# The low halves of the S5 layer's weights by an accumulating DMA instead of a VectorE subtraction

## The chip, the cores and the metric

The kernel runs on one core of one Trainium2 chip. The metric is the device time of one execution in microseconds. The kernel before takes 1155.73 us (median of 3 runs, 1154.44 to 1156.47).

## The reference

A trunk of four layers on 256 tokens of width 1024, all in float32. Each layer is a token mixer and then a SwiGLU feed-forward block, both behind an RMS norm and with a residual add. The mixers are forgetting attention (layer 0), a diagonal state-space layer called S5 (layer 1), multi-scale pooling (layer 2), and forgetting attention again (layer 3). Only layer 1 is touched here:

```python
def s5_layer(h, w_in, ..., w_glu):
    u = (h @ w_in).astype(F32)                      # 1024 x 1024
    bu = jnp.einsum('gpc,bsgc->bsgp', b_bar, u_g)   # 64 groups of 16 channels, 64 states each
    _, states = lax.associative_scan(combine, (lam_seq, bu), axis=1)
    y = jnp.einsum('gcp,bsgp->bsgc', c_mat, states).real.reshape(B, S, D_MODEL)
    g = jax.nn.gelu(y + d * u)
    val, gate = jnp.split(g @ w_glu, 2, axis=-1)    # 1024 x 2048
    return val * jax.nn.sigmoid(gate)
```

## The kernel before, in words

Activations lie with channels on the 128 partitions and the 256 tokens in the free dimension. TensorE multiplies in a fast float32 format (fp32r) that keeps fewer bits, so each operand is split into a rounded high half and a low half that holds the rest; a product is three matmuls: high by high, low by high, high by low (`term`).

All large weights stream through SBUF in **units** of 128 x 1024 float32 (512 KB), in one list over the whole program (`unit_list`). Each unit goes through three steps:

- `fetch` starts a DMA from SP's queue into one of 4 `raw` buffers;
- `split_unit` rounds `raw` on ScalarE into the first half of one of 5 `hl` buffers (the high half), and VectorE subtracts that half from `raw` into the second half (the low half);
- the matmuls on TensorE read `hl`.

`unit` is called when the code comes to the matmuls of a unit. It records the fetches up to 3 units ahead (`DMA_AHEAD`) and the splits up to 2 units ahead (`CAST_AHEAD`). A step can run only when its buffer is free: a `raw` buffer when the last reader of its former unit is done, an `hl` buffer when TensorE is done with the unit five places before.

The order of instructions on each engine is fixed when the program is built, by the language's scheduler, which may place an instruction ahead of others recorded before it; each engine then runs its list in order. Work between the matmuls (norms, the state-space steps) is put off by `at` and brought in by `tick`, which the matmul loops call.

The S5 layer has 24 units: 8 for `w_in` (`w_s5`), 4 for the first quarter of the GLU matrix (`w_glu0`, consumed while the state-space cores finish) and 12 for the rest of it (`w_glu1`). Units 0 and 1 are multiplied together, alternating over the 8 pieces of the inner dimension. While units 2 to 7 and the first GLU units are multiplied, eight state-space **cores** (`core`, `emit`) run between them: each needs three tables that an earlier preparation wrote to HBM (`E` 512 KB, `tab` 384 KB, `par` 768 KB, loaded by SP in `tables`), matmuls on TensorE (`e`, then `tp`) and eleven VectorE instructions on 256 to 512 elements. The last 12 units alternate value and gate: after each pair ScalarE takes the sigmoid of the gate, VectorE multiplies and adds to the residual, and `settled` makes the piece `X` and the squares `s` for the next norm.

Before the layer, the preparation of the tables ends in the feed-forward block of layer 0; its last pieces (`pe`, `pk`) leave through GpSimd's DMA queue. GpSimd also raises the norms' sums to the power -1/2 (L243) and loads the pooling layer's band matrix.

Of the kernel before, what the change touches and what calls it, by code (L numbers as in the profile page):

```python
# [9 lines left out]
F32 = mybir.dt.float32  # L10
F32R = mybir.dt.float32r
AF = mybir.ActivationFunctionType
ALU = mybir.AluOpType
# [13 lines left out]
CAST_AHEAD = 2  # L27
# [6 lines left out]
class Trunk:  # L34
# [21 lines left out]
    def units(self):  # L56
        a, u = self.a, []

        def ffn(l):
            for i in range(NCH):  # L60
                u.extend((a["w_gu"][l, i, 0], a["w_gu"][l, i, 1]))
            for d in range(8):
                u.extend(a["w_dn"][l, d][:, s] for s in (slice(0, 1024), slice(1024, 2048), slice(2048, 2816)))

        for l in range(self.layers):
            kind, j = l % 3, l // 3
            if kind == 0:
                u.extend(a["w_vf"][j, k] for k in range(8))
                for hp in range(8):
                    u.extend((a["w_qk"][j, hp, 0], a["w_qk"][j, hp, 1]))  # L70
                u.extend(a["w_fo"][j, k] for k in range(8))
            elif kind == 1:
                u.extend(a["w_s5"][m] for m in range(8))
                u.extend(a["w_glu0"][k] for k in range(4))
                u.extend(a["w_glu1"][d] for d in range(12))
            else:
                u.extend((a["w_pool"][:, 0:1024], a["w_pool"][:, 1024:2048]))
            ffn(l)
        self.unit_list = u
# [12 lines left out]
    def split_unit(self, h):  # L92
        nc = self.nc
        raw, cuts = self.raw.pop(h)
        hl = self.wp.tile([128, 2, 1040], F32R, tag="hl", name="hl", bufs=HL_BUFS)
        for p in range(len(cuts) - 1):
            s = slice(cuts[p], cuts[p + 1])
            nc.scalar.copy(hl[:, 0, s], raw[:, s])  # L98
            nc.vector.tensor_tensor(out=hl[:, 1, s], in0=raw[:, s], in1=hl[:, 0, s].bitcast(F32), op=ALU.subtract)  # L99
        self.hl[h] = hl  # L100

    def unit(self):
        h = self.used
        self.used += 1
        last = len(self.unit_list) - 1
        while self.fetched <= min(h + DMA_AHEAD - 1, last):
            self.fetch(self.fetched)
            self.fetched += 1
        while self.cast <= min(h + (CAST_AHEAD if h else 0), last):
            self.split_unit(self.cast)  # L110
            self.cast += 1
        return self.hl.pop(h)
# [905 lines left out]
```

## Time and profile before

| | |
|---|---|
| median of the runs | 1155.73 us |
| the profiled execution | 1157.62 us |
| its span, first to last instruction | 1155.8 us |
| TensorE, VectorE, ScalarE, GpSimd busy | 97%, 75%, 59%, 11% of the span |
| loads from SP's queue (hardware) | 200.86 MB, 54.3% of the 16 DMA engines |
| transfers from GpSimd's queue (software) | 22.00 MB, 5.8% |
| granted TensorE clock | 0.99 |

The S5 layer lies between about 341 and 450 us of the span. In the table of windows each engine has its busy time and, in brackets, its number of instructions; then come the granted clock, the mean busy share of the 16 DMA engines and what they moved in GB/s. In the rows of groups and of the timeline a line such as L99 is the line in the kernel's code; `hl<-raw,hl` names what is written and what is read; the last bracket tells how long the engine had been idle and what ended that. L156 is the helper through which all matmuls go.

### The profile page before, as it was taken

Reading aid. Unit: us, or ns where it says so; the run is one execution under the profiler, and the core shown is the slowest. Engines: PE = TensorE matmul, PEld = TensorE weight load, DVE = VectorE, ACT = ScalarE, POOL = GpSimd, SP = SyncE. Lnnn points to the kernel's source line nnn. Section 1 sums busy time; section 2 is a strip of 40 time slices with the busy share of each in tenths; the row PEclk is TensorE's granted clock in tenths of the full one; section 3 lists DMA queues with packets and bytes.
Section 4 is the critical chain, followed back from the end, with each engine's and each line's share of the span. In section 5 each row is a group of like instructions: output and inputs, shape, how many; then the busy total and the mean of one; then the engine's idle time right before and its main releaser. Section 6 shows DMA issues by size and latency. Waiting matters only on the chain. (4 is left out here: it accounts for less than half of the span.)

```text
span 1155.8 us, 22388 instructions
## 1 busy us (share of the span) xinstructions
PE 1119.3 (97%) x8706; PEld 1027.9 (89%) x8706; DVE 868.6 (75%) x1647; ACT 683.7 (59%) x1273; POOL 121.5 (11%) x167
## 2 busy tenths in 40 slices
PE   7979999999999999999999899999999999999997
PEld 6968999999999999888888888888898998888886
DVE  5979976798769975988756688876755667887763
ACT  5557755777753254766644676665545677666551
POOL 1176000111110000000000000000005720000000
PEclk9989999999999999999999999999999999999999
DMA  8654466788889744665566265556665544655661
GB/s 287 203 163 153 155 209 196 239 264 253 259 267 332 292 137 158 219 190 193 176 181 190 92 192 191 190 184 184 196 196 180 180 134 148 205 193 186 180 188 49
DMA packets 63210, 224.98 MB, mean 195 GB/s; under 512 B 7648, under 2 KB 7984, under 8 KB 62976
## 3 DMA queue, kind: packets, MB, share of 16 engines
q1 hardware_dynamic: 56368, 200.86, 54.3%
q0 software_dynamic: 6160, 22.00, 5.8%
q8 instruction: 68, 1.11, 0.4%
q10 hardware_dynamic: 576, 0.69, 0.2%
q14 instruction: 38, 0.31, 0.1%
HBM read 208.81 MB, written 14.71 MB: 193 GB/s over the span
## 5 line engine op out<-in xcount | busy, mean ns | idle before, releaser
L156 PE MATMUL P<-X,hl 128*128 128x256 f32 (+1 forms) x4560 | 678.1, 308 | 3.4 <-DVE t L183 2.0
L156 PEld LDWEIGHTS P<-X,hl 128*128 128x128 f32 x4560 | 618.2, 190 | 52.7 <-issue 6.9
L99 DVE TENSOR_TENSOR hl<-raw,hl 128x1024 fp32r<-128x1024 f32 (+3 forms) x363 | 434.7, 1199 | 143.0 <-ACT hl L98 134.9
L98 ACT CAST hl<-raw 128x1024 fp32r<-128x1024 f32 (+3 forms) x363 | 372.3, 1028 | 162.3 <-PE acc L156 75.5
L156 PE MATMUL acc<-H,hl 128*128 128x512 f32 (+1 forms) x1628 | 251.1, 315 | 0.0
L156 PEld LDWEIGHTS acc<-H,hl 128*128 128x128 f32 x1628 | 226.6, 188 | 21.1 <-issue 0.6
L182 ACT COPY lo<-P 128x256 f32<-128x256 f32 x126 | 46.8, 372 | 107.8 <-PE P L156 107.8
L183 DVE TENSOR_TENSOR t<-P,lo 128x256 f32<-128x256 f32 x126 | 53.2, 424 | 44.4 <-ACT lo L182 44.3
L156 PE MATMUL acc<-X,hl 128*128 128x256 f32 (+1 forms) x384 | 61.3, 300 | 0.1
L409 POOL TENSOR_SCALAR nb<-nb,c 128x128 f32<-128x128 f32 (+1 forms) x64 | 59.6, 945 | 1.1
L243 POOL TENSOR_TENSOR rs<-rs,mhalf 128x2 f32<-128x2 f32 x9 | 6.6, 735 | 469.5 <-DVE rs L242 469.5
L156 PEld LDWEIGHTS acc<-X,hl 128*128 128x128 f32 x384 | 50.5, 188 | 3.7 <-DVE X L194 0.3
L430 ACT ACTIVATE pt<-pt,st 128x128 f32<-128x128 f32 (+1 forms) x64 | 28.6, 448 | 24.5 <-DVE st L428 24.3
L278 ACT ACTIVATE t<-t 128x256 f32<-128x256 f32 x88 | 36.8, 419 | 8.1 <-DVE t L277 4.7
L156 PE MATMUL P<-hl,X 128*128 128x336 f32 (+1 forms) x192 | 40.4, 330 | 0.0
L208 ACT ACTIVATE X<-x,gains 128x256 fp32r<-128x256 f32 x55 | 27.7, 506 | 12.9 <-DVE x L263 12.3
L217 ACT ACTIVATE s<-x 128x256 f32<-128x256 f32 x63 | 25.6, 406 | 15.7 <-DVE x L263 13.1
L156 PEld LDWEIGHTS P<-hl,X 128*128 128x128 f32 x192 | 33.5, 197 | 0.0
L156 PE MATMUL acc<-hl,X 128*128 128x352 f32 x96 | 24.5, 338 | 8.6 <-DVE X L206 7.6
L209 DVE SCALAR_TENSOR_TENSOR X<-x,gains,X 128x256 fp32r<-128x256 f32 x56 | 26.8, 480 | 5.4 <-ACT X L208 5.3
L280 DVE TENSOR_TENSOR t<-t 128x256 f32<-128x256 f32 x66 | 28.0, 424 | 1.9
L277 DVE TENSOR_TENSOR t<-t,R 128x256 f32<-128x256 f32 x66 | 28.0, 424 | 1.7
(179 smaller groups left out, 852.9 us busy)
## 6 DMA issues: line engine op xcount, KB each, us to landing
raw<-in_w_gu SPq DMA_DIRECT2D x176, 512.0 KB, 3.7
raw<-in_w_dn SPq DMA_DIRECT2D x64, 512.0 KB, 3.7
raw<-in_w_qk SPq DMA_DIRECT2D x32, 512.0 KB, 3.6
raw<-in_w_dn SPq DMA_DIRECT2D x32, 384.0 KB, 3.2
raw<-in_w_fo SPq DMA_DIRECT2D x16, 512.0 KB, 4.3
raw<-in_w_glu SPq DMA_DIRECT2D x16, 512.0 KB, 5.5
raw<-in_w_vf SPq DMA_DIRECT2D x15, 520.0 KB, 4.3
nb<-nd POOLq DMA_DIRECT2D x24, 256.0 KB, 6.3
```

The source lines that it names most:

```text
L98: nc.scalar.copy(hl[:, 0, s], raw[:, s])
L99: nc.vector.tensor_tensor(out=hl[:, 1, s], in0=raw[:, s], in1=hl[:, 0, s].bitcast(F32), op=ALU.subtract)
L156: self.nc.tensor.matmul(out, lhsT=lhsT, rhs=rhs, start=start, stop=stop)
L182: nc.scalar.copy(lo, o[:, N:])
L183: nc.vector.tensor_tensor(out=t, in0=o[:, 0:N], in1=lo, op=ALU.add)
L208: nc.scalar.activation(self.X[:, d, 0], x, AF.Identity, scale=g)
L209: nc.vector.scalar_tensor_tensor(out=self.X[:, d, 1], in0=x, scalar=g, in1=self.X[:, d, 0].bitcast(F32), op0=ALU.mult, op1=ALU.subtract)
L277: nc.vector.tensor_tensor(out=t, in0=t if wide else G, in1=R, op=ALU.mult)
L278: nc.scalar.activation(t, t, AF.Silu)
L280: nc.vector.tensor_tensor(out=h, in0=h if wide else U, in1=t, op=ALU.mult)
L409: nc.gpsimd.tensor_scalar(out=nb[:, i], in0=nb[:, i], scalar1=self.c[t][:, 4 * n + i:4 * n + i + 1], scalar2=None, op0=ALU.add)
L430: nc.scalar.activation(pt, pt, AF.Exp, bias=st[:, 0:1], scale=-1.0, accum_out=st[:, 1:2])
```

## The change

For the 24 units of the S5 layer the low half is formed in another way. ScalarE rounds as before; then ScalarE writes the negated rounded half into the low half's place (an activation with scale -1); then GpSimd issues a DMA that adds the unit's raw weights, read once more from HBM, to what stands there. The subtraction on VectorE goes away for these units. Their splits are recorded 3 instead of 2 units ahead. For all other units nothing changes.

```diff
+        self.added = ()
         for l in range(self.layers):
...
                 u.extend(a["w_s5"][m] for m in range(8))
                 u.extend(a["w_glu0"][k] for k in range(4))
                 u.extend(a["w_glu1"][d] for d in range(12))
+                self.added = range(len(u) - 24, len(u))
...
             nc.scalar.copy(hl[:, 0, s], raw[:, s])
-            nc.vector.tensor_tensor(out=hl[:, 1, s], in0=raw[:, s], in1=hl[:, 0, s].bitcast(F32), op=ALU.subtract)
+            if h in self.added:
+                nc.scalar.activation(hl[:, 1, s], hl[:, 0, s].bitcast(F32), AF.Identity, scale=-1.0)
+                nc.gpsimd.dma_start(hl[:, 1, s], self.unit_list[h][:, s].bitcast(F32R), accum_op=ALU.add)
+            else:
+                nc.vector.tensor_tensor(out=hl[:, 1, s], in0=raw[:, s], in1=hl[:, 0, s].bitcast(F32),
+                                        op=ALU.subtract)
...
-        while self.cast <= min(h + (CAST_AHEAD if h else 0), last):
+        while self.cast <= min(h + (CAST_AHEAD + (self.cast in self.added) if h else 0), last):
```

The change also moves instructions. The code grows by seven lines, so L98 (rounding) becomes L100, L208 and L217 become L215 and L224, L243 becomes L250, L708 and L710 become L715 and L717, and L826 becomes L833; the negation is L102 and the accumulating DMA L103.

GpSimd at the layer's start, before. `pe` and `pk` are the last pieces of the tables, `sx` the cleared states, `rs` the norm's power, `band` the pooling matrix of the next layer.

```order
L718 DMA s5d7_88<-pe_4309 128x512
L710 DMA s5d7_88<-pk_2311 128x512
L782 MEMSET sx0_4509 128x8
L782 MEMSET sx1_4510 128x8
L243 TENSOR_TENSOR rs_4504<-rs_4504,mhalf_75 128x2
L470 DMA band_6096<-in_band 128x1088
```

And now; hl_4415, hl_4449, hl_4479, hl_4524 and hl_4530 are units 0 to 4.

```order
L725 DMA s5d7_88<-pe_4309 128x512
L103 DMA hl_4415<-in_w_s5 128x1024
L717 DMA s5d7_88<-pk_2311 128x512
L103 DMA hl_4449<-in_w_s5 128x1024
L103 DMA hl_4479<-in_w_s5 128x1024
L103 DMA hl_4524<-in_w_s5 128x1024
L789 MEMSET sx0_4515 128x8
L789 MEMSET sx1_4516 128x8
L250 TENSOR_TENSOR rs_4510<-rs_4510,mhalf_75 128x2
L103 DMA hl_4530<-in_w_s5 128x1024
```

The accumulations of units 0 to 3 now stand ahead of the norm's power, that of unit 1 behind the write of `pk`.

ScalarE at the same place, now (before, the rounding of unit 1 is followed by the same `pk` copies, `X` and `s`, and there are no negations):

```order
L100 CAST hl_4415<-raw_4410 128x1024
L102 ACTIVATE hl_4415<-hl_4415 128x1024
L100 CAST hl_4449<-raw_4447 128x1024
L715 COPY pk_2311<-tp_4386 32x4x32 x4
L215 ACTIVATE X_3700<-x_72,gains_74 128x256
L224 ACTIVATE s_4406<-x_72 128x256
L102 ACTIVATE hl_4449<-hl_4449 128x1024
L100 CAST hl_4479<-raw_4477 128x1024
L102 ACTIVATE hl_4479<-hl_4479 128x1024
```

The negation of unit 1 stands behind the copies of `pk` and the activations of the last pieces of the feed-forward block.

TensorE at the first pair of units, where `tp<-cst,sq` is the norm's sum and `tp<-cst,rs` spreads its result; before:

```order
L156 MATMUL P<-X,hl 128x256 x26
L156 MATMUL tp<-cst,sq 128x1 x2
L156 MATMUL P<-X,hl 128x256 x4
L249 MATMUL tp<-cst,rs 128x128 x2
L156 MATMUL P<-X,hl 128x256 x18
```

and now:

```order
L163 MATMUL P<-X,hl 128x256 x20
L163 MATMUL tp<-cst,sq 128x1 x2
L163 MATMUL P<-X,hl 128x256 x10
L256 MATMUL tp<-cst,rs 128x128 x2
L163 MATMUL P<-X,hl 128x256 x18
```

The norm's sum stands six matmuls earlier. Everywhere else the order of TensorE's instructions is the same as before.

## The prediction

> **What bounds the kernel now.** I read the stretch of the S5 layer first, in the view of busy time by windows, with cuts at the places where its work changes kind: the end of the feed-forward block before it, the first pair of weight units, two stretches with the state-space cores, the first GLU units, the last GLU units.
>
> ```profile
> core 0: us, PE busy (x) PEld busy (x) DVE busy (x) ACT busy (x) POOL busy (x), PEclk, DMA share, GB/s
> 320.00:341.00 21.00, 21.00 (x190) 20.67 (x189) 12.58 (x19) 11.60 (x18) 2.17 (x4) 1.00 0.82 250
> 341.00:352.00 11.00, 10.03 (x130) 9.38 (x129) 6.96 (x12) 4.20 (x6) 0.87 (x3) 1.00 0.96 363
> 352.00:372.00 20.00, 20.00 (x413) 18.93 (x411) 19.02 (x36) 6.43 (x8) 0.00 (x0) 1.00 0.88 304
> 372.00:395.00 23.00, 22.90 (x466) 21.47 (x468) 22.86 (x42) 7.10 (x10) 0.00 (x0) 1.00 0.96 357
> 395.00:415.00 20.00, 19.85 (x392) 18.49 (x389) 15.10 (x27) 6.46 (x10) 0.00 (x0) 1.00 0.39 130
> 415.00:450.00 35.00, 35.00 (x294) 34.82 (x294) 25.73 (x41) 21.39 (x36) 0.66 (x2) 1.00 0.55 170
> ```
>
> From 341 to 450, 109 us, TensorE is idle for 1.2 us in all. VectorE is nearly full from 352 to 395 (41.9 of 43 us), and so are the DMA engines from 341 to 395 (shares 0.96, 0.88, 0.96). ScalarE has room, GpSimd is idle. Which of the full ones sets the pace is told by what TensorE waits for, so I then read TensorE's waits from 325 to 455.
>
> ```profile
> PE tp L249 <- POOL rs L243: 0.9, 2, 0.5
> PE e L156 <- DVE u L789: 0.3, 1, 0.3
> PE tp L156 <- DVE sq L220: 0.2, 1, 0.2
> ```
>
> 1.4 us in all, at the norms' ends and once at the first core. TensorE does not wait for a subtraction (hl, L99) anywhere in the layer, though VectorE is full: VectorE keeps up. So there is almost nothing to win, and what matters is what the new form of the low half costs elsewhere.
>
> **The change part by part.**
>
> *Removed: 24 subtractions on VectorE.* The groups of 341 to 395 price one at 1.22 us, the ScalarE rounding beside it at 1.05 us.
>
> ```profile
> L99 DVE TENSOR_TENSOR hl<-raw,hl 128x1024 fp32r<-128x1024 f32 x10 | 12.1, 1221 | 2.5 <-ACT hl L98 2.4
> L98 ACT CAST hl<-raw 128x1024 fp32r<-128x1024 f32 x10 | 10.4, 1047 | 20.4 <-DMA raw<-in_w_s 7.5 <-PE acc L156 7.3 <-DMA raw<-in_w_glu 3.0
> ```
>
> 24 x 1.22 = 29 us leave VectorE, none of it on TensorE's path but one. At the first norm a subtraction stands ahead of the last X and sq.
>
> ```profile
> 342.36 1.23 DVE L99 TENSOR_TENSOR hl<-raw,hl 128x1024 fp32r<-128x1024 f32 x1
> 343.90 0.42 DVE L220 TENSOR_TENSOR sq<-sq,s 128x256 f32<-128x256 f32 x1
> 341.02 3.20 PE L156 MATMUL P<-X,hl 128*128 128x256 f32 x26
> 344.46 0.58 PE L156 MATMUL tp<-cst,sq 128*128 128x1 f32 x4 [0.23 <-DVE sq L220]
> 346.09 0.43 PE L249 MATMUL tp<-cst,rs 128*128 128x128 f32 x2 [0.47 <-POOL rs L243]
> ```
>
> Without it sq is ready up to 1.1 us sooner, and the new order puts the norm's sum after 20 matmuls instead of 26 and 10 behind it instead of 4, so the gaps of 0.23 and 0.47 can close: at best -0.7 us.
>
> *Added on ScalarE: 24 negations of 128x1024.* No such instruction is in the trace. These rows of the last GLU units bound it:
>
> ```profile
> 443.15 0.39 ACT L826 ACTIVATE s<-P 128x256 f32<-128x256 f32 x1 [1.75 <-PE P L156]
> 443.43 1.04 ACT L98 CAST hl<-raw 128x1024 fp32r<-128x1024 f32 x1
> 444.49 0.51 ACT L208 ACTIVATE X<-x,gains 128x256 fp32r<-128x256 f32 x1
> 444.90 0.40 ACT L217 ACTIVATE s<-x 128x256 f32<-128x256 f32 x1
> 446.02 1.05 ACT L98 CAST hl<-raw 128x1024 fp32r<-128x1024 f32 x1 [0.71 <-ACT s L217]
> 448.80 0.39 ACT L826 ACTIVATE s<-P 128x256 f32<-128x256 f32 x1 [1.74 <-PE P L156]
> ```
>
> An activation of 256 elements costs 0.40 or, with a vector as scale, 0.51; the rounding of 1024 costs 1.05. I take 1.05 (1.30 by the ratio 0.51 to 0.40). Over two GLU units (443.15 to 448.80, 5.65 us) ScalarE then holds 0.39 + 2 x 1.05 + 0.51 + 0.40 + 2 x 1.05 = 5.5 us: just enough, and 6.0 at the upper price, too much by 0.35 per pair.
>
> *Added on GpSimd and the DMA engines: 24 accumulating transfers.* Each reads the 512 KB of raw weights from HBM a second time, reads the 512 KB of the negated half, writes 512 KB. The trace has none, so I bound it by loads. Share and rate of a saturated stretch, 341 to 352:
>
> ```profile
> GB/s 432 343 75 0 223 60 119 149 179 402 410 372 439 391 413 436 480 380 402 402 462 402 402 417 402 432 454 365 391 425 451 413 369 458 458 425 358 425 492 402
> q1 hardware_dynamic: 990, 3.97, 95.0%
> ```
>
> The last 31 slices average 417 GB/s, so 0.524 MB take 1.26 us of all 16 engines; by busy share (95.0% of 11 us for 3.97 MB) 1.38 us. Lower bound for one accumulate: one such load. Upper: three, one for each stream. I take two, 2.5 to 2.8 us, since both operands must be read. The nearest rows for the time from issue to landing are GpSimd's own transfers:
>
> ```profile
> s5d<-cxv POOLq DMA_DIRECT2D x8, 512.0 KB, 4.5
> bc<-in_s_bc POOLq DMA_DIRECT2D x1, 1024.0 KB, 7.9
> ```
>
> 4.5 us is the lower end (same bytes written), 7.9 the one I take (the bytes read are the same).
>
> In the Trainium skill, Collectives: The Full Stack, section "The bandwidth ceiling: the fold count and why AG ≠ RS ≠ AR", a DMA that adds is said to run at half the rate of a copy, because it fetches two operands through the one read ring, the addition itself being free. No run shown so far tests it; it would give two loads per accumulate too, against one if only the bytes written counted.
>
> *The sum, first place: the S5 layer's start.* Units 0 and 1 feed one interleaved pair that starts at 341.02.
>
> ```profile
> 332.71 1.05 ACT L98 CAST hl<-raw 128x1024 fp32r<-128x1024 f32 x1 [1.07 <-PE acc L156]
> 335.17 0.40 ACT L217 ACTIVATE s<-x 128x256 f32<-128x256 f32 x1
> 335.58 0.54 POOL L710 DMA_DIRECT2D s5d<-pk  x1 [7.16 <-DVE pk L526]
> 345.32 0.72 POOL L243 TENSOR_TENSOR rs<-rs,mhalf 128x2 f32<-128x2 f32 x1 [3.91 <-DVE rs L242]
> ```
>
> Unit 1 is rounded at 332.71, but in the new order the four pk copies, X and s stand between its rounding and its negation: that runs 335.6 to 336.6, and GpSimd, in order, has pk's write (335.58) ahead of it. Issued at 336.6 it lands at 341.1 (4.5) or 344.5 (7.9); it is wanted at 341.4, three matmuls after 341.02. Late by 0 to 3.1 us, of which the 0.7 of gaps are taken back: -0.7 to +2.4, I take +2. The norm's power stays undisturbed: units 1 to 3 are issued ahead of it on GpSimd, the last at about 342, and it runs at 345.32.
>
> *Second place: DMA time from 341 to 450.* 21 accumulates fall here (24 less units 0 to 2). By bytes: 11 x 363 + 20 x 304 + 23 x 357 + 20 x 130 + 35 x 170 = 26.8 MB, 64.3 us at 417 GB/s; plus 42 x 1.26 = 52.9 makes 117.2 us of work in 109: 8 over. By busy share: 0.96 x 11 + 0.88 x 20 + 0.96 x 23 + 0.39 x 20 + 0.55 x 35 = 77.3, so 31.7 free against 42 x 1.38 = 58: 26 over. About 5 us can go past 450 (four raw buffers of 1.26). So +3 to +21. I take +7, nearer the low end, because the quoted slices swing between 358 and 492 GB/s under a full share: the share fills before the bytes do. It shows at two points. The tables' loads (E, tab, par) come late:
>
> ```profile
> 351.65 0.32 SPq L834 DMA_DIRECT2D E<-s5d  x1
> 361.18 2.01 PE L156 MATMUL e<-u,E 32*128 32x64 f32 x64
> E<-s5d SPq DMA_DIRECT2D x3, 512.0 KB, 6.3
> ```
>
> E is issued at 351.65 and wanted at 361.18, 9.5 us, against 6.3 to land (372 to 395): only 3 us spare. And the last GLU units: TensorE eats one in 2.85 us (below), the DMA engines need 1.26 + 2.5 = 3.8.
>
> ```profile
> 415.54 33.23 PE L156 MATMUL P<-X,hl 128*128 128x256 f32 x280
> 363.13 0.97 PE L156 MATMUL acc<-X,hl 128*128 128x256 f32 x6
> 366.21 3.10 PE L156 MATMUL acc<-X,hl 128*128 128x256 f32 x24
> 369.24 1.01 PE L156 MATMUL e<-u,E 32*128 32x64 f32 x28
> SPq L87 <- DVE hl L99: 62.0, 21, 7.0
> ```
>
> (33.23 / 280 x 24 = 2.85.) Casting one unit further ahead adds nothing here: five hl buffers hold the lead at four units either way. The last row is SP's wait for raw buffers; they now come free at the rounding, so raw loads start sooner, which costs nothing but meets the tables' loads.
>
> Sum: +2 + 7 = +9 us. The profiled execution took 1157.62 us (span 1155.8 and 1.8 around it) and would take 1166.6; it lies 1.9 above the median of the runs, 1155.73, so the forecast is 1164.7.
>
> **The rivals.**
>
> *Hidden, no change (0.27).* An accumulate costs the engines what a load costs: 21 x 1.38 = 29 of 31.7 us free, everything lands within its lead. For it: between two cores (361.18 to 369.24, 8.1 us) TensorE uses 6 + 24 = 30 matmuls of weights, 1.25 units, so a lead of four units is 26 us there. Against: shares of 0.96. Time: 1155.7 with -0.7 to +2 at the start, 1156.
>
> *ScalarE and latency in the last GLU units, DMA rate sufficient (0.12).* From the sigmoid at 443.15 a unit's rounding, X, s and negation end at 446.4; it is used four units later, at 443.15 + 11.4 = 454.5: 8.1 us for issue and landing. Landing in 10 us misses by 2, which a loop of four units turns into 0.5 per unit, 8 units: +4, 1159.7.
>
> *Three streams at full price (0.12).* 63 x 1.26 + 64.3 = 143.7 us of work in 109: 35 over, less 5, plus 2: 1188. For it: nothing shows how the engines add; it decides from 2.2 loads per accumulate on.
>
> *Faster: VectorE paces after all (0.06).* Between cores 24 matmuls occupy 366.21 to 369.24, 0.126 us each, against 33.23 / 280 = 0.119 later. If a full VectorE causes that, freeing it returns 240 x 0.0076 = 1.8 us (240 matmuls: units 2 to 7 and the first four GLU units), and with the 1.4 us of TensorE's waits 3.2: 1152.5. It decides if accumulates cost nothing. Against: no wait on VectorE is recorded there.
>
> **How the numbers follow.** Forecast 0.43, own range 1158 to 1179. The whole range takes in the hidden case below and most of the way to three streams above: 1155.2 to 1186. A measurement of this kernel tells about 0.2%, 2.3 us, from no change. Slower: 0.43 + 0.12 + 0.12 and 0.03 of the hidden case, 0.70. Same 0.24. Faster 0.06.
>
> **What would show it.** Right: TensorE waits for hl behind a DMA, first for unit 1 at about 341, then for E or tab between 360 and 400, then in the last GLU units; DMA share near 1 to 450; GpSimd's hl transfers 7 to 9 us to landing; VectorE's busy time down 29 us, ScalarE's up 25. Wrong: hl transfers landing in about 5 us at a DMA share that rises by no more than 0.3, with TensorE's waits unchanged (hidden), or landings far over 10 us (three streams).

## The result, and the profile after

The changed kernel takes 1188.75 us (median of 4 runs, 1188.11 to 1189.13) against 1156.1 us for the kernel before on the same chip: a ratio of 1.0284, with a 95% interval of 1.0266 to 1.0302. That is 32.6 us slower. The forecast was 9 us slower, and the range ended at 1186: the sign was right, the size 3.6 times too small.

The profiled execution took 1189.13 us, with a span of 1187.3 (before: 1157.62 and 1155.8). First the busy times and GpSimd's DMA queue, from the page of the kernel after; the columns of a queue are packets, MB and the share of 16 engines over the span.

```profile
PE 1129.9 (95%) x8706; PEld 1037.2 (87%) x8706; DVE 841.4 (71%) x1623; ACT 706.8 (60%) x1297; POOL 145.9 (12%) x191
q0 software_dynamic: 9616, 34.59, 11.0%
```

VectorE has 27 us less to do and ScalarE 23 us more (before: 868.6 and 683.7), as expected. GpSimd's queue moves 12.6 MB more, the 24 units, and its share of the span has nearly doubled, from 5.8 to 11.0%.

The same windows as before from 341 on, in the same columns, and one more, since the layer now ends at about 480:

```profile
341.00:352.00 11.00, 5.81 (x28) 5.60 (x29) 1.08 (x4) 1.92 (x4) 1.02 (x4) 0.69 1.05 288
352.00:372.00 20.00, 17.79 (x270) 17.02 (x268) 12.27 (x23) 7.67 (x8) 3.69 (x5) 0.83 1.04 331
372.00:395.00 23.00, 22.25 (x481) 20.79 (x480) 13.78 (x28) 9.02 (x12) 2.59 (x3) 1.00 1.04 344
395.00:415.00 20.00, 17.41 (x320) 16.41 (x312) 13.59 (x28) 8.31 (x10) 2.60 (x3) 0.91 1.04 336
415.00:450.00 35.00, 30.48 (x426) 28.99 (x415) 14.33 (x32) 20.61 (x30) 5.11 (x6) 0.95 0.72 184
450.00:482.00 32.00, 25.41 (x196) 23.71 (x195) 12.18 (x22) 17.45 (x27) 4.09 (x7) 1.00 0.96 267
```

Two columns at the right carry the finding. The DMA share stands at 1.04 to 1.05 from 341 to 415, yet the rate is 288 to 344 GB/s, where the kernel before moved 357 and 363 at a share of 0.96. The engines are full and move less. The clock column has fallen too, to 0.69 and 0.83 in the windows where TensorE waited most. Every other engine has room in every window.

TensorE's waits from 325 to 490, in us in total, times, and the longest:

```profile
PE P L163 <- DMA hl<-in_w_glu: 7.1, 8, 1.3
PE P L163 <- DMA hl<-in_w_s: 5.9, 2, 4.4
PE e L163 <- DMA E<-s5d: 4.5, 2, 2.6
PE acc L163 <- DVE X L201: 4.0, 1, 4.0
```

These are new, and all go back to DMAs: the low halves (hl), the table `E`, and, one step behind the wait for X, the table `tab`. VectorE, which makes X, had itself waited for `tab`, issued at 409.58 and landed 14.9 us later:

```profile
424.53 0.69 DVE L867 TENSOR_TENSOR A<-e,tab 128x512 f32<-128x512 f32 x1 [6.35 <-DMA tab<-s5d]
```

The timeline of TensorE shows where the waits sit; the bracket at the end is the idle time before the group.

```profile
341.78 0.63 PE L163 MATMUL P<-X,hl 128*128 128x256 f32 x3 [1.48 <-DMA hl<-in_w_s]
346.82 3.78 PE L163 MATMUL P<-X,hl 128*128 128x256 f32 x16 [4.41 <-DMA hl<-in_w_s]
...
361.76 3.65 PE L163 MATMUL e<-u,E 32*128 32x64 f32 x64 [1.96 <-DMA E<-s5d]
...
400.83 2.01 PE L163 MATMUL e<-u,E 32*128 32x64 f32 x64 [2.59 <-DMA E<-s5d]
...
429.51 2.03 PE L163 MATMUL acc<-X,hl 128*128 128x256 f32 x10 [4.00 <-DVE X L201]
...
437.57 10.67 PE L163 MATMUL P<-X,hl 128*128 128x256 f32 x89
448.72 3.10 PE L163 MATMUL P<-X,hl 128*128 128x256 f32 x24 [0.47 <-DMA hl<-in_w_glu]
...
476.97 2.98 PE L163 MATMUL P<-X,hl 128*128 128x256 f32 x23 [0.79 <-DMA hl<-in_w_glu]
479.79 0.86 PE L163 MATMUL acc<-X,hl 128*128 128x512 f32 x4
```

Two rows of before to set beside them, the first core and the end of the last GLU units (their start, at 415.54, is in the prediction):

```profile
349.57 2.01 PE L156 MATMUL e<-u,E 32*128 32x64 f32 x64 [0.26 <-DVE u L789]
448.60 0.86 PE L156 MATMUL acc<-X,hl 128*128 128x512 f32 x4
```

The loss grows in three places. The first core starts at 356.06 instead of 349.57: 6.5 us late, after the two waits for unit 1. The last GLU units start at 437.57 instead of 415.54: 22.0 us late, so 15.5 us came between, while cores and first GLU units ran. They end at 479.79 instead of 448.60: 31.2 late, so another 9.2 came there. The last eight of them, one unit each, arrive every (476.97 - 448.72) / 7 = 4.04 us, where TensorE would take 2.85.

Not all of that is waiting. After a long wait the same matmuls take longer: 16 take 3.78 us after 346.82, where 26 took 3.20 in the same pair before, and 64 small ones (`e`) take 3.65 at 361.76, where the first core of before took 2.01. At 400.83, behind a wait of 2.59, they still take 2.01, and the slowness comes 2 us later. The granted clock shows it:

```profile
362.00:368.00 6.00, 6.00 (x76) 5.88 (x75) 3.96 (x9) 1.15 (x2) 0.00 (x0) 0.50 1.05 287
403.00:406.00 3.00, 3.00 (x12) 2.82 (x13) 1.45 (x3) 1.52 (x2) 0.00 (x0) 0.50 1.04 281
```

Read in narrow windows, it stands at 0.50 in four stretches, from about 344.8, 361.9, 402.8 and 430.1, for 6.8, 6.8, 3.4 and 3.4 us. TensorE is at work for all but 2 of these 20.4 us; at half speed that is an estimated loss of about 9 us. The sum over the eight groups from 346 to 433 that are longer than their like gives about 9 too. TensorE's waits are about 21 us more than before. The two together are 30 of the 31.5 us by which the span grew.

### The profile page after: what moved, and what is told of

Same layout as the page of the kernel before. It is cut to its first block, busy times and chain, and to the rows that moved or that the text cites. A ratio compares the mean times of both kernels' runs of the same rounds, so it can differ in the third digit from the quotient of the medians.

```text
span 1187.3 us, 22421 instructions
## 1 busy us (share of the span) xinstructions
PE 1129.9 (95%) x8706; PEld 1037.2 (87%) x8706; DVE 841.4 (71%) x1623; ACT 706.8 (60%) x1297; POOL 145.9 (12%) x191
## 4 chain that ended last, share of the span: by engine, by line
PE 55%; DMA 1%; DVE 1%; issue 1%; POOL 1%; ACT 1%; POOLq 0%; DVEq 0%; ACTq 0%
PE P L163 35%; PE acc L163 18%; DMA hl<-in_w_glu 1%; PE tp L163 1%; DVE hl L105 0%; PE tp L453 0%; ACT hl L100 0%; POOL nb L416 0%; POOL nb L412 0%; DMA nd<-nct 0%; PE tp L470 0%; PE tp L256 0%; DVE t L190 0%; POOL rs L250 0%; DVE xg L901 0%
## 5 line engine op out<-in xcount | busy, mean ns | idle before, releaser
L163 PE MATMUL P<-X,hl 128*128 128x256 f32 (+1 forms) x4560 | 682.1, 309 | 16.4 <-DMA hl<-in_w_glu 7.1
L105 DVE TENSOR_TENSOR hl<-raw,hl 128x1024 fp32r<-128x1024 f32 (+3 forms) x339 | 405.3, 1197 | 135.8 <-ACT hl L100 128.2
L100 ACT CAST hl<-raw 128x1024 fp32r<-128x1024 f32 (+3 forms) x363 | 372.0, 1028 | 161.6 <-PE acc L163 83.1
L163 PE MATMUL acc<-X,hl 128*128 128x256 f32 (+1 forms) x384 | 64.0, 310 | 4.0 <-DVE X L201 4.0
L250 POOL TENSOR_TENSOR rs<-rs,mhalf 128x2 f32<-128x2 f32 x9 | 6.6, 734 | 472.3 <-DVE rs L249 472.3
L163 PEld LDWEIGHTS acc<-X,hl 128*128 128x128 f32 x384 | 53.1, 198 | 7.6 <-DVE X L201 4.2
L215 ACT ACTIVATE X<-x,gains 128x256 fp32r<-128x256 f32 x55 | 27.7, 504 | 13.8 <-DVE x L270 13.2
L224 ACT ACTIVATE s<-x 128x256 f32<-128x256 f32 x63 | 25.6, 406 | 15.3 <-DVE x L270 13.1
```

The costliest lines, as they stand in the source:

```text
L163: self.nc.tensor.matmul(out, lhsT=lhsT, rhs=rhs, start=start, stop=stop)
L215: nc.scalar.activation(self.X[:, d, 0], x, AF.Identity, scale=g)
```

## The experiments

The first theory, A, was made of this trace: an accumulating transfer holds the DMA engines for as long as two loads, and the engines' time is what runs out. The rivals put the loss on other things that came in with the change: the longer chain of steps and its landing time, ScalarE's new work, GpSimd's queue, or the second read of the weights from HBM. Except where said otherwise an experiment is an edit of the kernel after. Its ratio is to the kernel before, run on the same chip.

### The same transfers without the addition

```diff
-                nc.gpsimd.dma_start(hl[:, 1, s], self.unit_list[h][:, s].bitcast(F32R), accum_op=ALU.add)
+                nc.gpsimd.dma_start(hl[:, 1, s], self.unit_list[h][:, s].bitcast(F32R))
```

> The changed kernel with one difference: GpSimd's transfer copies the raw weights over the negated half instead of adding them (so the low half is wrong; same queue, same bytes from HBM, same places in every engine's order). Theory A, engine time: in the trace of the change an accumulate holds the 16 DMA engines 2.7 us, twice a load's 1.37; a copy should hold them 1.4, and the layer then needs 77 + 29 of its 109 us: +0 to +6 us against before (1156 to 1162), TensorE's waits for hl gone from the last GLU units. Theory B, the longer path of a unit (negation, GpSimd issue, landing, in-order places on ScalarE): the path is the same, so the loss stays, +25 us or more. Theory C, the second reading of the weights from HBM: it is still read, so the loss stays, +25 us or more.

Measured: 1161.17 us, ratio 1.0037 (1.0025 to 1.0049), 4.4 us slower than before. Queue, number and size of the transfers and ScalarE's work are those of the kernel after; only the addition is gone, and 28 of the 32.6 us go with it. The queue on the page, then two windows:

```profile
q0 software_dynamic: 9616, 34.59, 9.0%
```

```profile
341.00:352.00 11.00, 9.42 (x96) 9.21 (x96) 2.05 (x5) 3.86 (x6) 1.25 (x2) 0.84 1.05 412
372.00:395.00 23.00, 23.00 (x477) 21.82 (x474) 21.12 (x43) 10.61 (x14) 2.11 (x4) 1.00 1.05 410
```

At the same share of 1.05 the engines now move 410 GB/s instead of 288 and 344. The price of one transfer follows from the queue's share of the span. Before, GpSimd's queue held 5.8% of 1155.8 = 67.0 us without these transfers; so one plain copy costs (0.090 x 1160.0 - 67.0) / 24 = 1.56 us of all 16 engines, and one accumulate (0.110 x 1187.3 - 67.0) / 24 = 2.65 us. Theory A holds; the theories without the addition in them, which wanted 25 us or more here, fall.

### The addition from the raw buffer instead of HBM

```diff
-                nc.gpsimd.dma_start(hl[:, 1, s], self.unit_list[h][:, s].bitcast(F32R), accum_op=ALU.add)
+                nc.gpsimd.dma_start(hl[:, 1, s], raw[:, s].bitcast(F32R), accum_op=ALU.add)
```

> The changed kernel with the accumulating DMA reading the raw weights from the raw buffer in SBUF instead of a second time from HBM. Theory A: two operands are still read through the DMA engines, 2.7 us per unit: the loss stays, +28 to +38 us (a raw buffer is also held until the addition has landed, which can add some). Theory B: the same. Theory C: HBM is read once only, so most of the loss goes, +0 to +8 us.

Measured: 1188.05 us, ratio 1.0265 (1.0240 to 1.0289), the whole loss. The weights are no longer read twice from HBM, and the price is the same: (0.111 x 1187.8 - 67.0) / 24 = 2.70 us. (The waits lie elsewhere: 11.0 us for `E`.)

```profile
q0 software_dynamic: 9616, 34.59, 11.1%
```

The second read of HBM is not the cause.

### The negation kept, the subtraction back on VectorE

```diff
-                nc.gpsimd.dma_start(hl[:, 1, s], self.unit_list[h][:, s].bitcast(F32R), accum_op=ALU.add)
+                nc.vector.tensor_tensor(out=hl[:, 1, s], in0=raw[:, s], in1=hl[:, 0, s].bitcast(F32),
+                                        op=ALU.subtract)
```

> The negation on ScalarE and the splits one unit further ahead stay, but the low half is then written by VectorE's subtraction as before; no DMA is added. Theory A and C: nothing is left that costs, 1155 to 1157.5 us. Theory B: ScalarE's extra 25 us and its changed order are part of the path and cost at least +3 us, above all in the last GLU units.

Measured: 1159.32 us, ratio 1.0023 (1.0007 to 1.0039). ScalarE has all its new work and the order of the splits is the new one, and 2.5 us are lost, slightly more than A allowed. Nothing of it is in the last GLU units, where theory B looked for it first:

```profile
416.65 33.23 PE L164 MATMUL P<-X,hl 128*128 128x256 f32 x280
```

ScalarE is busy there for 28.58 of 35 us, and the 280 matmuls take 33.23 us, to the hundredth what they took before. The 2 us come earlier: TensorE stands still for 1.3 us ahead of the second core, at 354.05, and for 0.4 at 366.69, in neither case behind anything that the profile shows, and for 0.7 at 410.21 behind an X of VectorE. Their cause was not found.

### Half the units: every second, the last twelve, the first twelve

Three ways to take half of the accumulates, in this order:

```diff
-                self.added = range(len(u) - 24, len(u))
+                self.added = range(len(u) - 23, len(u), 2)
```

```diff
-                self.added = range(len(u) - 24, len(u))
+                self.added = range(len(u) - 12, len(u))
```

```diff
-                self.added = range(len(u) - 24, len(u))
+                self.added = range(len(u) - 24, len(u) - 12)
```

> Every second of the 24 units is formed by the accumulating DMA, the others by VectorE's subtraction. Theory A: 12 x 2.74 = 33 us of DMA time against 31.7 us free: the engines are just full instead of far over, so the loss is far less than half, +2 to +9 us (1158 to 1165). Theory B or C: a cost per unit, so about half of 32.6: +14 to +18 us.

> Only the last 12 units (the rest of the GLU matrix) are formed by the accumulating DMA; the others as before. In the trace of the change the last GLU stretch grew by 9.2 us (31.2 late at its end against 22.0 at its start). Theory A, engine time: per unit one load (1.37) and one accumulate (2.74) make 4.1 us where TensorE needs 2.85; the stretch pays about as in the change, +7 to +11 us, since its overload is its own. If the overload were mostly carried in from the core stretch, it pays much less, +0 to +4 us.

> Only the first 12 units (w_in and the first quarter of the GLU matrix) are formed by the accumulating DMA. Theory A: the start and the core stretch pay as in the change, 22 us late at the first of the last GLU units, of which the accumulations for later units (about 3 of 11 in that time) are taken away: +14 to +22 us. If the two halves of the layer don't act on each other, this run and the last-12 run add up to 32.6.

| units that accumulate | time, us | ratio (interval) | loss, us |
|---|---|---|---|
| every second | 1161.35 | 1.0038 (1.0026 to 1.0051) | 4.4 |
| the last twelve | 1167.43 | 1.0097 (1.0071 to 1.0123) | 11 |
| the first twelve | 1172.71 | 1.0137 (1.0109 to 1.0166) | 16.4 |
| all | 1188.75 | 1.0284 (1.0266 to 1.0302) | 32.6 |

The same number of transfers costs 4.4 us spread out and 11 or 16.4 in a row. A fixed cost for each would have given half of the loss, 16, wherever they stand. So it is a budget that overflows. With every second unit the last GLU units run without a gap, since two units then need 1.38 x 2 + 2.65 = 5.4 us of the engines and TensorE eats them in 5.7. With all twelve in a row the budget per unit is 1.38 + 2.65 = 4.03 us, and the units arrive every (455.00 - 426.84) / 7 = 4.02. TensorE waits there eight times, 7.2 us in all.

The first and the last twelve make 27.5 us together, 5 less than all 24. Each of the three is known to within 2 or 3 us, so this 5 is hardly clear of the noise. That the first half leaves the second with less of a lead would explain it, but was not shown.

### Without the first four units

```diff
-                self.added = range(len(u) - 24, len(u))
+                self.added = range(len(u) - 20, len(u))
```

> Units 0 to 3 are formed by VectorE's subtraction as before, the other 20 by the accumulating DMA. In the trace of the change TensorE waits 1.5 and 4.4 us for units 0 and 1, and the norm's R comes that much later: the layer's first pair takes 14.9 us instead of 7.4. If the start is a cost of its own, it goes, and with it 4 x 2.74 us of DMA work: 32.6 - 7.5 = +25 us or less, down to +15 if the tables that were late had been held up by those four. If the engines' overload is what counts in the end and the start only moved it forward, +28 us or more.

Measured: 1183.07 us, ratio 1.0226 (1.0202 to 1.0250), 26.8 us slower, between the two expectations. The 6 us stall for unit 1 is gone. But 20 accumulates still cost 27 of 33 us, and TensorE waits 5.9 us for `E`, up to 4.0 at a time.

So the first four accumulates cost about 6 us. How much of that is the stall for unit 1 and how much their share of the engines' time, this run does not separate.

### One more unit of lead

```diff
-DMA_AHEAD = 4
-HL_BUFS = 5
+DMA_AHEAD = 5
+HL_BUFS = 6
...
-        while self.cast <= min(h + (CAST_AHEAD + (self.cast in self.added) if h else 0), last):
+        while self.cast <= min(h + (CAST_AHEAD + 2 * (self.cast in self.added) if h else 0), last):
```

> The changed kernel with six hl buffers instead of five, and splits and fetches recorded one unit further ahead: the lead of a unit grows from four units to five. Theory A, engine time: the last GLU units still come at the rate of the DMA engines, about 4.0 us each (as in the change), and the total stays within 5 us of the change, +27 to +33 us. Theory L, latency of the path: four units per 16.1 us is the loop's length, and with five in it a unit takes 16.1 / 5 = 3.2 us: the last stretch loses only 3 us instead of 9, total +20 to +26 us.

Measured: 1179.42 us, ratio 1.0194 (1.0168 to 1.0220), 23 us slower than before and 9 faster than the kernel after. The total fell where the theory of landing time had it, and the detail that tells the two apart went the other way. In the last GLU units, TensorE's waits come every (471.15 - 455.11) / 4 = 4.01 us, where more lead against a landing time would have given 3.2:

```profile
PE e L163 <- DMA E<-s5d: 10.4, 2, 5.4
PE P L163 <- DMA hl<-in_w_glu: 3.9, 5, 1.5
```

It is a rate. The sixth buffer only holds more finished units when the last GLU units start: five waits instead of eight. The stall for unit 1 is gone too, and part of it comes back as a longer wait for `E`.

### One accumulate alone

```diff
-                self.added = range(len(u) - 24, len(u))
+                self.added = range(len(u) - 11, len(u) - 10)
```

> Only one unit, the second of the last 12, is formed by the accumulating DMA; it is issued near 400 us, where the engines' share before was 0.39. It shows the price of one accumulate with little beside it. Theory A: it holds the 16 engines about 2.7 us (0.524 MB on GpSimd's queue) and lands in 5 to 7 us; the total is that of before within 2 us. If the 2.7 us were an effect of the crowded engines, it holds them about 1.4 us, as a load does.

Measured: 1155.97 us in one execution, beside 1156.35 before. The one transfer is issued at 394.51. The queues in the 7 us in which it ran, 396 to 403:

```profile
q0 software_dynamic: 144, 0.52, 49.3%
q1 hardware_dynamic: 146, 0.52, 24.2%
```

It lands 8.0 us after its issue (the view of the tile `hl`). It holds the engines for 49.3% of 7 us = 3.45 us, while the same bytes of loads beside it take 24.2% = 1.69. Both of its numbers are above what theory A said, but the factor of two is there with the engines at a mean share of 0.76, so the crowd isn't what makes an accumulate dear.

### A gap at the same place, without any DMA

In the kernel before, the low half of unit 1 of the layer (number 101) is formed late: GpSimd subtracts it four times over.

```diff
+            if h == 101:
+                for _ in range(4):
+                    nc.gpsimd.tensor_tensor(out=hl[:, 1, s], in0=raw[:, s], in1=hl[:, 0, s].bitcast(F32),
+                                            op=ALU.subtract)
+                continue
```

> The kernel before, with no added DMA: only the low half of unit 1 is written by GpSimd, four times over, so that it comes some microseconds late for the first pair of the layer and TensorE has to wait there, as it does in the changed kernel. Theory G, the gap itself lowers TensorE's granted clock: after a wait of 4 us or more the next 16 or so matmuls take about 0.24 us each instead of 0.12, as behind the 4.4 us wait of the change, and the total grows by the wait and 2 to 3 us more. Theory D, those matmuls were slow because of the crowded DMA engines or late data: they run at 0.12 to 0.13 at once, and the total grows by the wait alone.

Measured: 1161.89 us, ratio 1.0051 (1.0035 to 1.0068). TensorE's group after the gap, then the window behind it:

```profile
341.48 4.40 PE L161 MATMUL P<-X,hl 128*128 128x256 f32 x22 [2.55 <-POOL hl L101]
```

```profile
341.00:345.00 4.00, 3.52 (x19) 3.53 (x20) 3.96 (x5) 0.53 (x2) 0.51 (x3) 0.66 0.60 195
```

The wait is 2.55 us, and the 22 matmuls behind it take 0.20 us each instead of 0.12, another 1.7 us, at a granted clock of 0.66. The DMA engines are at 0.60 here, so it isn't they that slow the matmuls: it is the gap. Waits of half a microsecond to 1.3 in the last GLU units of the kernel after don't do this; there the clock reads 1.00. Around two microseconds the length of the wait alone doesn't decide: the clock fell to 0.50 behind waits of 1.83 us (without the first four units), 1.96 (the kernel after) and 2.46 (the copy), and stayed at 1.00 behind 2.10 (every second unit), 2.23 (from the raw buffer) and 2.40 (the next experiment).

The Trainium skill, TensorE: Matmul & The Clock Gate, section "Part 1: The HAM clock gate (the "warmup" mystery)", has the clock fall to half after an idle window of about 3.4 us and come back after about 3.4 us of work. The runs agree on the way back: the stretches at 0.50 last 3.4 us here, and 3.4 or 6.8 in the kernel after. On the way down they have waits of 1.83 to 2.55 us that were followed by slow matmuls, shorter than the page's figure.

### The subtraction on GpSimd

An edit of the kernel before, for 22 units; no DMA is added.

```diff
-            nc.vector.tensor_tensor(out=hl[:, 1, s], in0=raw[:, s], in1=hl[:, 0, s].bitcast(F32), op=ALU.subtract)
+            e = nc.gpsimd if 102 <= h < 124 else nc.vector
+            e.tensor_tensor(out=hl[:, 1, s], in0=raw[:, s], in1=hl[:, 0, s].bitcast(F32), op=ALU.subtract)
```

> The kernel before, with the subtractions of units 2 to 23 of the layer on GpSimd instead of VectorE: VectorE is relieved of 22 x 1.22 = 27 us as in the change, but no transfer is added. A GpSimd subtraction takes 2.45 us (two took 4.9 in the run with the late unit 1), less than TensorE needs for a unit. Theory W, there was nothing to win from VectorE: 1154.5 to 1158, no change that can be measured. Theory V, VectorE set TensorE's pace in the core stretch: the 3.2 us of the prediction's faster case come back, 1151 to 1154.

Measured: 1169.07 us, ratio 1.0099 (1.0070 to 1.0127). Neither expectation holds; it is a bad way to relieve VectorE, and why is told under what was not expected.

### No subtraction and no DMA

```diff
-                nc.gpsimd.dma_start(hl[:, 1, s], self.unit_list[h][:, s].bitcast(F32R), accum_op=ALU.add)
```

> The changed kernel without the accumulating DMA: the negated half is left as the low half (the addition of the raw weights is left out, so the low half is wrong). VectorE is relieved of all 24 subtractions, GpSimd and the DMA engines get nothing, ScalarE keeps the negations. This is the most that taking the subtractions off VectorE could bring. Theory W, nothing to win: 1154.5 to 1158.5, the negations' order costing what it did in the run with negation and subtraction (+2.5 at most). Theory V, VectorE set TensorE's pace in the core stretch: 1151 to 1154, and the time from one core's first matmul to the next core's falls below 8.06 us.

Measured: 1155.9 us (12 runs), ratio 0.9997 (0.9984 to 1.0011). With the addition free, this is what moving the subtraction off VectorE could bring in this order of instructions.

```profile
372.00:395.00 23.00, 22.60 (x483) 21.17 (x485) 16.02 (x32) 10.94 (x14) 0.00 (x0) 1.00 0.94 323
```

```profile
393.29 2.01 PE L162 MATMUL e<-u,E 32*128 32x64 f32 x64
...
398.31 3.11 PE L162 MATMUL acc<-X,hl 128*128 128x256 f32 x24
401.34 2.01 PE L162 MATMUL e<-u,E 32*128 32x64 f32 x64
...
414.84 33.23 PE L162 MATMUL P<-X,hl 128*128 128x256 f32 x280
```

VectorE's load falls from 22.86 to 16.02 of 23 us, and TensorE's rows get no shorter: 8.05 us from core to core here (8.06 before, from 361.18 to 369.24), and 42.3 us over the last five such steps (40.9 before); 24 matmuls in 3.11 us (3.10 before), 280 in 33.23. A full VectorE cost this kernel nothing that can be measured: by the interval, at most 0.2%.

## Why the prediction was right, and where it was wrong

**What bounds the kernel: right.** It said that TensorE waits for no subtraction and that there is almost nothing to win. With only the negation in its place the time is the same to 0.03%, with an interval of 0.16 below to 0.11 above. The rival in which VectorE paces after all had the one prop that 24 matmuls take 3.03 us between cores and less later; they still do with VectorE at 58% of the window (398.31 to 401.34; 11.59 of the 20 us from 395 to 415), so that is not VectorE's doing.

**The price of an accumulate: right.** Two loads were taken, 2.5 to 2.8 us, out of one to three; 2.65 and 2.70 were measured. The rule quoted beside it from the Trainium skill, Collectives: The Full Stack, section "The bandwidth ceiling: the fold count and why AG ≠ RS ≠ AR", that a DMA that adds runs at half the rate of a copy, agrees roughly: 2.65 us against 1.56 for the copy in the same place and 1.38 for a load. The landing time of 7.9 us was taken from another GpSimd transfer; alone, an accumulate lands in 8.0, and in the crowd in 9.6 (median), up to 15.0. The negation was taken at 1.05 us and takes 1.057 (median of 24). The landing in the view of the tile `hl` of the kernel after, from 325 to 490:

```profile
DMA to landing us min/median/max: 5.3/9.6/15.0
```

**The second place: the failed step.** The term "DMA time from 341 to 450" was worked out twice, 8 us over by bytes and 26 over by busy share, and 7 was taken on the ground that "the share fills before the bytes do". About 24.7 us were lost behind the start (31.2 - 6.5). The price per transfer was right; the room left for it was not. The quoted slices of 358 to 492 GB/s were read as spare room under a full share, with 417 GB/s as capacity. The copies show what a full share is worth with no accumulate in it: 410 GB/s at 1.05, so 390 at 1.00. At that rate the 26.8 MB of before take 68.7 us, and 21 accumulates at 2.65 another 55.7: 15.4 over the 109 us at a share of 1.00, and only 9.5 at the 1.05 that the engines reached. Much of the loss is then room that was there and wasn't used: in the windows after, from 341 to 482, shares times lengths add up to 133 us, where these 141 us at 1.05 could have held 148. The clearest place is 415 to 437, where TensorE waits 4.0 us for X and frees no hl buffer; its window, and the busy digits of the DMA engines:

```profile
415.00:437.00 22.00, 17.95 (x322) 16.66 (x311) 9.09 (x19) 8.41 (x11) 1.74 (x2) 0.92 0.75 202
DMA  9999999999999999997441869796799950000000
```

The digits divide 415 to 437 into 40 slices of 0.55 us: seven at the end are empty. At a mean share of 0.75 this window alone leaves at least 22 x 0.25 = 5.5 us unused. How the loss divides between too much work and unused room is an estimate; that the price was right is measured. The lead that the buffers hold when the last GLU units begin is then four units, and the eight behind them came at the engines' 4.03 us each instead of 2.85: 8 x 1.18 = 9.4, measured 9.2. The budget by busy share, 26 over (24 with 2.65 as the price), came nearer, in part by luck: it takes the loads of the quiet windows at the share that they had there (170 GB/s at 0.55, so 309 at 1.00 against 390), and that surplus stood in for the unused room. With "about 5 us" for work past 450 taken off, even its upper end of +21 fell short of the 24.7.

The places were named rightly: "the tables' loads come late", and 3.8 us for a unit in the last GLU units where TensorE needs 2.85. How late the tables come was not worked out. The prediction had 9.5 us from the issue of `E` to its use, against 6.3 to land. In the stretch of the cores (341 to 395 before, 341 to 415 after) the median from issue to landing went from 5.6 us to 13.5:

```profile
E<-s5d SPq DMA_DIRECT2D x8, 512.0 KB, 5.6
E<-s5d SPq DMA_DIRECT2D x7, 512.0 KB, 13.5
```

So the 3 us that it called spare were gone, and late tables (`E`, and `tab` behind X) are what TensorE waited for between the cores.

**The first place: too small.** +2 was taken, 0 to 3.1 us late for unit 1. It was issued early, at 335.76 instead of the 336.6 reckoned, but landed at 346.82, after 11 us: units 0 to 3 and the tables went through the engines at once, and "7.9" was the time of a transfer in a quieter place. The first core starts 6.5 us late, though the pair begins 1.0 sooner. The 0.7 us of gaps that should come back did come back where no unit was late: without subtraction and DMA the stretch from the pair to the first core is 7.82 us (339.67 to 347.49) instead of 8.55.

**A term that was missing.** No step of the prediction has TensorE slower after it has waited. The windows of before showed a clock of 1.00 throughout, and no wait long enough to tell. It is worth about 9 us here; the experiment with one late unit shows the effect itself, while the 9 us are an estimate from rows and the clock of the kernel after. That the kernel would be 9 us faster without it is not shown: where the DMA engines set the pace, a faster TensorE would have waited instead.

**The rivals.** "Three streams at full price" has 1188, the measured number, and is wrong: it needs 3 x 1.26 = 3.8 us for a transfer, and 2.65 was measured. It used the same budget by bytes; a price too high and a room too large nearly cancelled. "ScalarE and latency" falls twice: with ScalarE's work alone the last GLU units take the same 33.23 us, and a longer lead leaves 4.01 us per unit. "Hidden" is nearly what the copy shows: at 1.56 us per transfer 4.4 us were lost, 2.5 of them in one wait for unit 1 and about 1.7 in the slow matmuls behind it; no run has transfers at the 1.38 of a load.

**What stays open.** The 2.5 us with the negation and the subtraction both in place; the 5 us, hardly clear of the noise, by which all 24 cost more than the two halves; and how much of the loss between the cores is waiting and how much the clock, since the two come together.

## What to carry to other kernels

A full engine is worth relieving only if something waits for it: VectorE was at 99% for 23 us and cost nothing that could be measured, while the DMA engines, at 96% beside it, had little to lend. Price a transfer by the engines' busy share, not its bytes, and count only room that the buffers let it use: an accumulate of 512 KB counts as 0.52 MB in the rate and holds the engines like about 1.0. Where transfers come late, reckon also with some microseconds of matmuls at half speed behind waits of about two microseconds and more.

## What the runs showed of the hardware that was not expected

**A full share hides a low rate.** From 448 to 470 of the kernel after, in the last GLU units:

```profile
q0 software_dynamic: 819, 2.98, 69.1%
q1 hardware_dynamic: 787, 2.90, 35.3%
```

The two queues move the same bytes; the accumulates take twice the time, 69.1% of 22 us for 2.98 MB, 2.67 us per 0.524 MB, against 1.40 for a load. In the window from 341 to 352 the rate fell to 288 GB/s at a share of 1.05.

**GpSimd's arithmetic slows VectorE.** With the subtraction on GpSimd (2.52 us each), VectorE's instructions in that stretch took up to nearly three times as long. Groups of 341 to 400, GpSimd's subtractions on, then the kernel before; the numbers behind the bar are busy us and mean ns:

```profile
L869 DVE TENSOR_TENSOR C<-A,tab 128x512 f32<-128x512 f32 x6 | 8.1, 1350 | 0.2
L872 DVE TENSOR_TENSOR sx<-C,B 128x252 f32<-128x252 f32 x6 | 6.7, 1124 | 0.1
```

```profile
L868 DVE TENSOR_TENSOR C<-A,tab 128x512 f32<-128x512 f32 x7 | 4.8, 692 | 0.2
L871 DVE TENSOR_TENSOR sx<-C,B 128x252 f32<-128x252 f32 x6 | 2.5, 417 | 0.1
```

692 became 1350 ns, 417 became 1124, and TensorE waited 8.2 us for VectorE (from 325 to 465) where before it waited 0.5. Taking work from VectorE to GpSimd made VectorE the bound that it had not been. The Trainium skill, SBUF — State Buffer, section "Who interferes with whom", says that a tensor_tensor with both inputs in SBUF contends with GpSimd's reads; the rows agree, and give the size for these shapes.
